# Two pair steps moved ahead of a short convolution, and one operand split per gate tile in place of two, in a two-layer gated-mixer trunk

## The chip, the cores and the metric

The kernel runs on one core of a Trainium2 chip. The metric is the device time of one execution in microseconds (us); three executions of the kernel before gave a median of 1846.69 us.

## What is computed

The state x is 2048 tokens by 1024 features, float32. Layer 0 applies the short-convolution mixer, layer 1 a pooling mixer; after each mixer comes a gated embedding, and a last RMSNorm ends the trunk.

```
h  = rmsnorm(x, g)
b, c, v, z = split(h @ w_in, 4)                    # w_in 1024 x 4096
y  = b * causal_conv3(c * v, w_conv)               # three taps over the tokens, per feature
x  = x + (silu(z) * y) @ w_out                     # first mixer
gate = sigmoid(rmsnorm(x, g2) @ w_gate)
x  = x + gate * (p[0] @ w_proj)                    # gated embedding
...                                                # second mixer and its gate, then the last norm
```

## The kernel before

Features lie on the 128 partitions, tokens along the free dimension. There are four chunks of 512 tokens; `sc` = 0 and 1 handle two chunks each, through all of both layers (line 945 on). So the order of stages is: first mixer (`mixer_a`), its output product, two gates, second mixer (`mixer_b`), its output product, two gates, and all of that once more for `sc` = 1. What stands between the last gates of `sc` = 0 and the first mixer of `sc` = 1 is called the turn.

Every float32 product is made of three matmuls (`mm`, lines 273 to 275): high part of the weight by high part of the operand, high by low, low by high. High and low parts are made in advance: ACT casts a tile to its high part, DVE subtracts it from the tile. For a weight granule of 128x1024 that is lines 116 and 117 (`split_raw`), for an operand lines 301 and 302 (`split_act`) or 307 and 308 (`split_scaled`).

The first mixer's input product is done in the Strassen-Winograd manner over 2x2 blocks (two chunks of tokens, two halves of the features): seven products of sums in place of eight. The seven operand sums are x11, x21, t2, t1, t3, x22 and t4, each in four tiles. `X(name)` (class `Operands`, line 526) returns the four tiles of one and makes those that are still missing; `X.ahead(n)` makes the next n tiles in the order x11, x21, t2, t1, t3, x22, t4. For `sc` = 1 a tile is made by `second_operand` (line 604): `fetch` (lines 599 to 601) loads it from DRAM (`ndr`) into one of the four `n` buffers, and `split_act` splits it into one of the 31 `act` buffers. The `n` buffers also take the embedding tiles of the gates (`pdr`, line 748).

`pair_steps` (line 436) makes two output tiles of the product in three steps, with products of 12 matmuls each:
- step 1: x11 into PSUM tile pa, x21 into pb; ACT copies pa (c1, line 428), DVE adds pb and c1 (m1, line 433)
- step 2: t2 on top of pa, ACT copies pa again (c2); t1 into pc, ACT copies pc (c5)
- step 3: t3 on top of pa, DVE adds pa and c5 (n2); x22 on top of pc, DVE adds pc and c2 (m2); t4 on top of pa

In `mixer_a` (line 467) a loop runs over eight tiles j of 128 features. Each has a c-v pair and a z-b pair. In the program's order, tile j does: steps 2 and 3 of its c-v pair (line 479; step 1 was issued by the tile before, line 505); the products u1 and u2 of c and v (lines 483 and 484, on POOL and DVE); the convolution cv1 and cv2 (line 491 on ACT, then two taps each at line 493 on DVE); every other tile, the sums over the outputs of the two tiles before (`Y.add`, line 498, `combine`); all three steps of its z-b pair (line 502); step 1 of the next c-v pair (line 505); in `sc` = 0 some preparation of sums of the output weights (line 507); the gating (lines 511 to 516). u, cv, c1, m1, c2, c5, n2 and m2 all lie in the ten `wk` buffers.

What sets the order: nothing is ordered by hand but the program itself. The framework hands out the buffers of a pool strictly in the program's order (the first writers of the 784 `wk` tiles stand in that order in the compiled kernel before, without an exception), and within this and the data's own dependences its scheduler puts each engine's instructions in the order in which they become ready by its own reckoning, the earlier in the program first where several are ready. So c1 of the z-b pair, whose buffer comes after those of u2, cv1 and cv2, stands behind the first instruction of cv1 and cv2 in ACT's order, though the product that it copies is done long before. Each engine then runs its list in order. There are seven PSUM banks for products, and four weight granules in the ring `w` (loaded three ahead, `next_granule`, line 262).

In a gate (`gate`, line 770) each of eight tiles k has a product of 24 matmuls, an embedding tile from DRAM, `gate_out` (lines 752 to 755: DVE, ACT, DVE, DVE) and the squares for the next norm (line 328 on ACT, 331 on POOL), and then calls `extra(k)`; for the second layer's gates of `sc` = 0 that is `ahead` (line 970). Behind the second of these gates comes `filler` (line 984), embedding products of chunk 2, whose PSUM tiles are copied on ACT at line 735.

Of the kernel before, what the change touches and what calls it, by code (L numbers as in the profile page):

```python
# [48 lines left out]
def trunk_kernel(ctx: ExitStack, tc: tile.TileContext, xT, xN, pT, wts, par, out):  # L49
# [15 lines left out]
    def wtile():  # L65
        return wk.tile([P, 528], F32, tag="wk", name="wk")
# [5 lines left out]
    def pcol(c):  # L72
        return par_sb[:, c:c + 1]
# [69 lines left out]
    def prepare_sums(layer, i):  # L143

        base = (W_AOUT, W_BOUT)[layer] + 2 * i
        with tc.issue_after(newest[0].ins):
            w11, w12, w21, w22 = (fetch(wts[base + r][:, c * HK:(c + 1) * HK]) for r in range(2) for c in range(2))
        vec(w22, w21, w22, ALU.add)
        vec(w21, w11, w21, ALU.subtract)
        vec(w11, w22, w11, ALU.subtract)  # L150
        vec(w12, w12, w11, ALU.subtract)
        for n, sm in enumerate((w22, w11, w21, w12)):
            nc.sync.dma_start(out=so_dram[layer][:, n, i, :], in_=sm)
# [151 lines left out]
    def split_scaled(h, gcol):  # L305
        a = new_act()
        nc.scalar.activation(out=a[:, 0, :], in_=h, func=AF.Copy, scale=pcol(gcol))  # L307
        nc.vector.scalar_tensor_tensor(out=a[:, 1, :], in0=h, scalar=pcol(gcol), in1=a[:, 0, :].bitcast(F32),  # L308
                                       op0=ALU.mult, op1=ALU.subtract)
        return a  # L310
# [125 lines left out]
    def pair_steps(sc, i, X):  # L436

        pa, pb = psum(), psum()
        w = next_granule(("sum", (sc, i, 0)))
        product(pa, w, 0, X("x11"), True)  # L440
        product(pb, w, HK, X("x21"), True)
        c1 = copied(pa)
        m1 = added(pb, c1)
        yield
        w = next_granule(("sum", (sc, i, 1)))
        product(pa, w, HK, X("t2"), False)
        c2 = copied(pa)
        pc = psum()
        product(pc, w, 0, X("t1"), True)
        c5 = copied(pc)  # L450
        yield
        w = next_granule(("sum", (sc, i, 2)))
        product(pa, w, 0, X("t3"), False)
        n2 = added(pa, c5)
        product(pc, w, HK, X("x22"), False)
        m2 = added(pc, c2)
        w = next_granule(("sum", (sc, i, 3)))
        product(pa, w, 0, X("t4"), False)
        yield m1, m2, pa, n2

    def pair_of(steps):

        for r in steps:
            if r:
                return r

    def mixer_a(sc, X, Y, later):
        def steps(j, i):
            return pair_steps(sc, 2 * j + i, X)

        cv_steps = steps(0, 0)
        due = []
        for j in range(KT):
            zb_steps = steps(j, 1)
            if j == 0:
                next(cv_steps)
                next(zb_steps)
                look[0] = LOOK
            cs1, cs2, v1, v2 = pair_of(cv_steps)
            us = []  # L480
            for t, (c, v) in enumerate(((cs1, v1), (cs2, v2))):
                u = wtile()
                nc.gpsimd.tensor_copy(out=u[:, 0:2], in_=uh[:, j, :] if t == 0 else us[0][:, T:T + 2])
                nc.vector.tensor_tensor(out=u[:, 2:2 + T], in0=v, in1=c, op=ALU.mult)
                us.append(u)
            if sc == 0:
                nc.gpsimd.tensor_copy(out=uh[:, j, :], in_=us[1][:, T:T + 2])
            cvs = []
            for u in us:
                cv = wtile()  # L490
                nc.scalar.activation(out=cv[:, :T], in_=u[:, 0:T], func=AF.Copy, scale=pcol(C_CONV + j))
                for t in (1, 2):
                    nc.vector.scalar_tensor_tensor(out=cv[:, :T], in0=u[:, t:t + T],
                                                   scalar=pcol(C_CONV + 8 * t + j),
                                                   in1=cv[:, :T], op0=ALU.mult, op1=ALU.add)
                cvs.append(cv)
            for args in due:
                Y.add(*args)
            due = []
            if j == KT - 1:  # L500
                Y.begin(later)
            z1, z2, b1, b2 = pair_of(zb_steps)
            if j + 1 < KT:
                cv_steps = steps(j + 1, 0)
                next(cv_steps)
            for i in () if sc else ((), (0,), (1,), (2,), (3,), (4, 5), (6, 7), ())[j]:
                prepare_sums(*divmod(i, KT // 2))
            for t, (z, b) in enumerate(((z1, b1), (z2, b2))):
                cv = cvs[t][:, :T]
                zs = wtile()[:, :T]  # L510
                nc.scalar.activation(out=zs, in_=z, func=AF.Sigmoid)
                nc.vector.tensor_tensor(out=zs, in0=z, in1=zs, op=ALU.mult)
                nc.vector.tensor_tensor(out=cv, in0=cv, in1=zs, op=ALU.mult)
                if j % 2 == t == 0:
                    yt = [acts.tile([P, 2, T], F32, tag="act", name="y") for _ in range(2)]
                nc.vector.tensor_tensor(out=yt[t][:, j % 2, :], in0=b, in1=cv, op=ALU.mult)
            if j % 2:
                due.append((j // 2, yt))
        for args in due:
            Y.add(*args)  # L520
# [29 lines left out]
    def first_operand(x, stats):  # L550

        def make(name, kk):
            n11, n12, n21, n22 = (x[t][2 * kk + r] for r in range(2) for t in range(2))
            if name == "x11":
                normed(n11, n11, 2 * kk, stats[0].rb)
                return split_act(n11)
            if name == "x21":
                normed(n21, n21, 2 * kk + 1, stats[0].rb)
                return split_act(n21)
            if name == "t2":  # L560
                normed(n12, n12, 2 * kk, stats[1].rb)
                normed(n22, n22, 2 * kk + 1, stats[1].rb)
                vec(n12, n22, n12, ALU.subtract)
                vec(n11, n12, n11, ALU.add)
                return split_act(n11)
            if name == "t1":
                vec(n21, n21, n11, ALU.subtract)
                vec(n11, n22, n11, ALU.subtract)
                return split_act(n11)
            return split_act({"t3": n12, "x22": n22, "t4": n21}[name])  # L570
        return make
# [166 lines left out]
    def filler(layer, ch, *between):  # L738

        keys = filler_order(layer, ch)  # L740
        pt = next_granule(keys[0])
        for h in range(2):
            ple_half(layer, ch, pt, next_granule(keys[1 + h]), h)
            for f in between[h:h + 1]:
                f()
# [167 lines left out]
    X = Operands(first_operand(x, stats))  # L913
# [31 lines left out]
    for sc in range(2):  # L945
        chs = (2 * sc, 2 * sc + 1)
        Y = Outputs(2 * sc, (0, 1, 2, 3))
        mixer_a(sc, X, Y, xT[chs[1]])
        filler(*((0, 3) if sc else (1, 0)))
        a, hs, s = mixer_out(0, Y, xT[chs[0]])  # L950
        hooks.extend([s[1].fin1, nop, s[1].fin2])
        ab, ss = ([], []), []
        for t, ch in enumerate(chs):
            def after_gate(k):
                ab[t].append(split_scaled(hs[t][k], G_MIX + 8 + k))
                keep(ch, hs[t], k)

            ss.append(gate(0, ch, a[t], hs[t], s[t], after_gate))
            if t == 0:
                hooks.extend([ss[0].fin1, nop, ss[0].fin2])  # L960
        filler(1, 1 + sc, ss[1].fin1, ss[1].fin2)

        Y = Outputs(2 * sc + 1, (3, 2, 1, 0))
        mixer_b(ab, ss, Y, sc, nop if sc else between_b, h_dram[chs[1]])
        a, hs, s = mixer_out(1, Y, h_dram[chs[0]])
        hooks.extend([s[1].fin1, nop, s[1].fin2])
        if sc == 0:
            X = Operands(second_operand)

        def ahead(k):  # L970
            if sc == 0:
                X.ahead(1 + t)

        for t, ch in enumerate(chs):
            if ch == NCH - 1:
                look[0] = 1
                gate_last(1, ch, a[t], hs[t], s[t])
                break
            g = gate(1, ch, a[t], hs[t], s[t], ahead)
            if t == 0:  # L980
                hooks.extend(finals(ch, hs[t], g))
                continue
            fin1, _, fin2 = finals(ch, hs[t], g)
            filler(0, 2, fin1, fin2)
# [55 lines left out]
```

## Time and profile before

| | us |
|---|---|
| median of three runs | 1846.69 (1844.87 to 1856.14) |
| the profiled execution | 1848.54 |
| its span, first to last instruction | 1846.8 |
| PE busy in the span | 1776.5 |
| DVE busy in the span | 1350.7 |

PE does the matmuls, PEld loads their weights, DVE is the vector engine, ACT the scalar engine, POOL the third elementwise engine, SP only issues DMAs. An L with a number is a line of the kernel. Matmuls overlap: one of 512 columns is shown with 0.39 us, while the next starts 0.23 us after it; so what PE loses at a wait is read from the idle time that the profile gives for it and from the distance of the starts. A name behind an arrow (<-) in square brackets or at the end of a line is what ended the wait.

### The profile page before, as it was taken

Reading aid. Unit: us, or ns where it says so; the run is one execution under the profiler, and the core shown is the slowest. Engines: PE = TensorE matmul, PEld = TensorE weight load, DVE = VectorE, ACT = ScalarE, POOL = GpSimd, SP = SyncE. Lnnn points to the kernel's source line nnn. Section 1 sums busy time; section 2 is a strip of 40 time slices with the busy share of each in tenths; the row PEclk is TensorE's granted clock in tenths of the full one; section 3 lists DMA queues with packets and bytes.
Section 4 is the critical chain, followed back from the end, with each engine's and each line's share of the span. In section 5 each row is a group of like instructions: output and inputs, shape, how many; then the busy total and the mean of one; then the engine's idle time right before and its main releaser. Section 6 shows DMA issues by size and latency. Waiting matters only on the chain.

```text
span 1846.8 us, 22147 instructions
## 1 busy us (share of the span) xinstructions
PE 1776.5 (96%) x8014; PEld 1459.0 (79%) x8014; DVE 1350.7 (73%) x1878; ACT 754.6 (41%) x1141; POOL 233.3 (13%) x218
## 2 busy tenths in 40 slices
PE   8799999989999999999979999999999999999996
PEld 6587777878788888887868877877878888888796
DVE  4886776776988778879786555466698876578975
ACT  6642333344656221345553233234465511135542
POOL 1000000000322010013210000000032300001320
PEclk9999999999999999999999999999999999999998
DMA  9545455667355456853674434246635522265431
GB/s 322 191 146 195 168 205 186 243 232 272 114 194 187 146 198 221 281 198 127 209 239 155 137 103 137 94 146 221 246 126 194 192 109 99 97 224 170 142 114 47
DMA packets 122495, 324.49 MB, mean 176 GB/s; under 512 B 13584, under 2 KB 15632, under 8 KB 122384
## 3 DMA queue, kind: packets, MB, share of 16 engines
q1 hardware_dynamic: 122384, 323.06, 50.8%
q8 instruction: 63, 1.03, 0.2%
q14 instruction: 48, 0.39, 0.1%
HBM read 225.49 MB, written 97.52 MB: 175 GB/s over the span
## 4 chain that ended last, share of the span: by engine, by line
PE 65%; DVE 17%; issue 5%; DMA 5%; ACT 3%; POOL 1%; SPq 1%; DVEq 0%; ACTq 0%; POOLq 0%
PE mm L275 22%; PE mm L273 21%; PE mm L274 21%; DVE w L117 5%; DVE act L302 2%; DMA n<-ndr 2%; DMA n<-in_wts_dram 2%; DVE act L308 2%; ACT w L116 1%; DVE h L699 1%; DMA raw<-in_wts_dram 1%; DVE wk L754 1%; DVE n L548 1%; SPq L601 1%; ACT wk L428 1%
## 5 line engine op out<-in xcount | busy, mean ns | idle before, releaser
L273 PE MATMUL mm<-act,w 128*128 128x512 f32 (+1 forms) x2464 | 942.2, 385 | 19.5 <-ACT wk L428 10.8
L275 PE MATMUL mm<-act,w 128*128 128x512 f32 (+1 forms) x2464 | 935.0, 384 | 12.2 <-DVE w L117 12.0
L274 PE MATMUL mm<-act,w 128*128 128x512 f32 (+1 forms) x2464 | 943.7, 383 | 0.0
L273 PEld LDWEIGHTS mm<-act,w 128*128 128x128 f32 x2464 | 464.2, 188 | 121.3 <-ACT wk L428 16.6
L275 PEld LDWEIGHTS mm<-act,w 128*128 128x128 f32 x2464 | 463.2, 188 | 108.4 <-DVE w L117 17.7
L274 PEld LDWEIGHTS mm<-act,w 128*128 128x128 f32 x2464 | 464.4, 188 | 90.5 <-issue 0.5
L116 ACT CAST w<-raw 128x1024 fp32r<-128x1024 f32 (+1 forms) x283 | 281.6, 1002 | 563.2 <-PE mm L275 474.7
L117 DVE TENSOR_TENSOR w<-raw,w 128x1024 fp32r<-128x1024 f32 (+1 forms) x283 | 336.6, 1194 | 130.8 <-ACT w L116 127.2
L331 POOL TENSOR_TENSOR acc<-acc,wk 128x512 f32<-128x512 f32 x97 | 142.9, 1474 | 490.4 <-ACT wk L328 490.4
L433 DVE TENSOR_TENSOR wk<-mm,wk 128x512 f32<-128x512 f32 x96 | 65.8, 686 | 100.5 <-PE mm L275 100.5
L308 DVE SCALAR_TENSOR_TENSOR act<-h,par_sb,act 128x512 fp32r<-128x512 f32 x96 | 103.8, 1084 | 19.9 <-ACT act L307 17.9
L328 ACT ACTIVATE wk<-h 128x512 f32<-128x512 f32 (+1 forms) x126 | 75.3, 600 | 93.6 <-DVE h L755 93.2
L307 ACT ACTIVATE act<-h,par_sb 128x512 fp32r<-128x512 f32 x96 | 68.9, 718 | 72.7 <-DVE h L699 72.7
L699 DVE TENSOR_TENSOR h<-mm,h 128x512 f32<-128x512 f32 x112 | 75.9, 682 | 26.7 <-PE mm L275 20.7
L302 DVE TENSOR_TENSOR act<-n,act 128x512 fp32r<-128x512 f32 x112 | 76.3, 710 | 22.8 <-ACT act L301 22.7
L428 ACT COPY wk<-mm 128x512 f32<-128x512 f32 x96 | 53.0, 585 | 94.9 <-PE mm L275 94.9
L301 ACT CAST act<-n 128x512 fp32r<-128x512 f32 x112 | 65.7, 619 | 57.3 <-DMA n<-ydr 27.6
L669 DVE TENSOR_TENSOR wk<-wk 128x526 f32<-128x526 f32 (+5 forms) x80 | 55.5, 693 | 2.4
L352 POOL TENSOR_TENSOR r<-ms,nhalf 128x8 f32<-128x8 f32 x18 | 33.1, 1837 | 186.5 <-DVE ms L350 186.5
L684 ACT ACTIVATE wk<-wk 128x512 f32<-128x512 f32 x32 | 20.2, 630 | 78.0 <-DVE wk L682 77.9
L753 ACT ACTIVATE wk<-wk 128x512 f32<-128x512 f32 (+1 forms) x72 | 41.3, 579 | 21.6 <-DVE wk L752 21.4
L682 DVE TENSOR_TENSOR wk<-mm,rb 128x512 f32<-128x512 f32 x32 | 22.0, 688 | 37.6 <-PE mm L275 37.6
(124 smaller groups left out, 1296.1 us busy)
## 6 DMA issues: line engine op xcount, KB each, us to landing
raw<-in_wts_dram SPq DMA_DIRECT2D x154, 512.0 KB, 3.4
n<-ydr SPq DMA_DIRECT2D x84, 256.0 KB, 4.5
ydr<-y SPq DMA_DIRECT2D x32, 512.0 KB, 3.3
raw<-in_wts_dram SPq DMA_DIRECT2D x64, 256.0 KB, 3.3
raw<-sdo SPq DMA_DIRECT2D x32, 512.0 KB, 6.3
raw<-sda SPq DMA_DIRECT2D x32, 512.0 KB, 3.7
pdr<-wk SPq DMA_DIRECT2D x56, 256.0 KB, 4.0
n<-pdr SPq DMA_DIRECT2D x56, 256.0 KB, 3.5
```

The costliest lines, as they stand in the source:

```text
L116: nc.scalar.copy(out=hi[:, c], in_=raw[:, c])
L117: eng.tensor_tensor(out=lo[:, c], in0=raw[:, c], in1=hi[:, c].bitcast(F32), op=ALU.subtract)
L273: nc.tensor.matmul(out=ps, lhsT=wh, rhs=ah, start=first, stop=False, skip_group_check=skip)
L274: nc.tensor.matmul(out=ps, lhsT=wh, rhs=al, start=False, stop=False, skip_group_check=skip)
L275: nc.tensor.matmul(out=ps, lhsT=wl, rhs=ah, start=False, stop=last, skip_group_check=skip)
L302: nc.vector.tensor_tensor(out=a[:, 1, :], in0=y, in1=a[:, 0, :].bitcast(F32), op=ALU.subtract)
L307: nc.scalar.activation(out=a[:, 0, :], in_=h, func=AF.Copy, scale=pcol(gcol))
L308: nc.vector.scalar_tensor_tensor(out=a[:, 1, :], in0=h, scalar=pcol(gcol), in1=a[:, 0, :].bitcast(F32), op0=ALU.mult, op1=ALU.subtract)
L328: nc.scalar.activation(out=sq, in_=h, func=AF.Square)
L331: (eng or nc.gpsimd).tensor_tensor(out=acc, in0=acc, in1=sq, op=ALU.add)
L428: nc.scalar.copy(out=c, in_=ps)
L699: nc.vector.tensor_tensor(out=hs[t][k], in0=ps, in1=hs[t][k], op=ALU.add)
```

## The change

In `mixer_a`, behind the products u1 and u2 and ahead of the convolution, step 1 and step 2 of the z-b pair are issued (for the first tile step 2 alone, since its step 1 was issued before the loop's body); line 502 then runs what is left, step 3. In the second layer's gates of `sc` = 0, `ahead` makes one operand tile for each gate tile in both gates; before, it made one in the first gate and two in the second. So 16 of the 28 tiles are made there in place of 24; the four of t3 and the four of x22 are made when step 3 of the first c-v pair of `sc` = 1 asks for them, as the four of t4 were before.

```diff
@@ mixer_a @@
             if sc == 0:
                 nc.gpsimd.tensor_copy(out=uh[:, j, :], in_=us[1][:, T:T + 2])
+            if j:
+                next(zb_steps)
+            next(zb_steps)
             cvs = []
             for u in us:
                 cv = wtile()
@@ trunk_kernel @@
         def ahead(k):
             if sc == 0:
-                X.ahead(1 + t)
+                X.ahead(1)
```

## Rows read from the trace of the kernel before

**Rows 1.** The page, part 1: busy time, share of the span, instructions

```profile
PE 1776.5 (96%) x8014; PEld 1459.0 (79%) x8014; DVE 1350.7 (73%) x1878; ACT 754.6 (41%) x1141; POOL 233.3 (13%) x218
```

**Rows 2.** Busy time by stretch: PE, PEld, DVE, ACT, POOL (instructions), clock, DMA

```profile
105.00:400.00 295.00, 282.11 (x1217) 226.47 (x1217) 212.16 (x302) 99.98 (x141) 20.26 (x23) 1.00 0.57 201
...
850.00:965.00 115.00, 104.08 (x445) 83.68 (x444) 94.31 (x127) 61.27 (x95) 27.59 (x19) 0.99 0.62 204
965.00:1280.00 315.00, 307.52 (x1336) 250.48 (x1335) 175.89 (x236) 106.05 (x155) 8.30 (x17) 0.99 0.41 137
...
600.00:700.00 100.00, 100.00 (x439) 82.05 (x438) 71.55 (x114) 24.98 (x36) 8.49 (x14) 1.00 0.51 180
```

**Rows 3.** Waits of PE, 105 to 405 us: us, times, longest us

```profile
PE mm L273 <- ACT wk L428: 5.8, 8, 2.2
PE mm L275 <- DVE w L117: 5.7, 7, 2.1
PE mm L273 <- ACT w L116: 1.4, 3, 0.5
```

**Rows 4.** Waits of PE, 965 to 1280 us

```profile
PE mm L273 <- ACT wk L428: 5.1, 5, 2.8
PE mm L273 <- ACT w L116: 2.3, 5, 0.5
```

**Rows 5.** Timeline of ACT, 148 to 160 us: start, us, instruction, idle before

```profile
148.46 1.05 ACT L116 CAST w<-raw 128x1024 fp32r<-128x1024 f32 x1 [3.64 <-PE mm L275]
149.91 1.34 ACT L491 ACTIVATE wk<-wk,par_sb 128x512 f32<-128x512 f32 x2 [0.41 <-DVE wk L484]
151.15 0.56 ACT L428 COPY wk<-mm 128x512 f32<-128x512 f32 x1
159.06 1.07 ACT L428 COPY wk<-mm 128x512 f32<-128x512 f32 x2 [7.35 <-PE mm L275]
```

**Rows 6.** Timeline of PE, the same stretch

```profile
149.56 0.50 PE L273 MATMUL mm<-act,w 128*128 128x512 f32 x1 [0.46 <-ACT w L116]
...
150.36 0.39 PE L274 MATMUL mm<-act,w 128*128 128x512 f32 x1
151.60 0.50 PE L275 MATMUL mm<-act,w 128*128 128x512 f32 x1 [0.85 <-DVE w L117]
...
159.70 0.50 PE L273 MATMUL mm<-act,w 128*128 128x512 f32 x1 [0.50 <-ACT wk L428]
```

**Rows 7.** Timeline of PE, last tile of the first mixer, second time

```profile
1267.87 0.79 PE L273 MATMUL mm<-act,w 128*128 128x512 f32 x1 [2.84 <-ACT wk L428]
1268.46 0.63 PE L274 MATMUL mm<-act,w 128*128 128x512 f32 x1
1268.88 0.63 PE L275 MATMUL mm<-act,w 128*128 128x512 f32 x1
```

**Rows 8.** Waits of PE at the turn, 905 to 965 us

```profile
PE mm L273 <- ACT wk L735: 5.1, 1, 5.1
PE mm L273 <- DVE wk L752: 3.8, 2, 2.0
```

**Rows 9.** Timeline of ACT at the turn

```profile
936.18 0.62 ACT L301 CAST act<-n 128x512 fp32r<-128x512 f32 x1 [2.71 <-DMA out_dram<-h]
...
945.02 0.62 ACT L301 CAST act<-n 128x512 fp32r<-128x512 f32 x1 [3.11 <-DMA n<-ndr]
...
959.70 2.03 ACT L735 COPY wk<-mm 128x512 f32<-128x512 f32 x4
```

**Rows 10.** Durations ns (min/median/max) by line: the second half of an operand's split; a tap of the convolution

```profile
L302 DVE TENSOR_TENSOR act<-n,act x27: 676/683/1414, 859.8 to 962.9; 128x512 fp32r<-128x512 f32 x27
...
L493 DVE SCALAR_TENSOR_TENSOR wk<-wk,par_sb x32: 734/742/753, 115.8 to 396.9; 128x512 f32<-128x512 f32 x32
```

**Rows 11.** Timeline of DVE, behind the first boundary of rows 5

```profile
161.11 1.22 DVE L117 TENSOR_TENSOR w<-s,w 128x1024 fp32r<-128x1024 f32 x1 [5.11 <-ACT w L116]
```

## The prediction, made before the changed kernel was run

> **What bounds the kernel now.** I read the page first: PE is busy for 1776.5 of 1846.8 us, 96%, so nothing but PE's lost time can be won [rows 1]. Busy time hides part of the loss, so I next read the kernel by stretches and counted matmuls. In 600 to 700 us PE never waits and starts 439 matmuls, one in 0.228 us. At that rate 105 to 400 us (first mixer, first time) would hold 1294; it holds 1217, so some 77, or 17.6 us, are missing. The turn (850 to 965) misses 59, 13.5 us; the first mixer's second time (965 to 1280) misses 46, 10.5 us [rows 2]. A few records may be lacking, so these are upper bounds: some 41 us lie in the stretches that the change touches, and the other stages matter little.
>
> The waits of PE say what ends these stops. In the first mixer it waits for three things: an ACT copy of PSUM (line 428), the low part of a weight granule (DVE, line 117), and its high part (ACT, line 116): 5.8, 5.7 and 1.4 us in the first time [rows 3], 5.1, none and 2.3 us in the second [rows 4]. The timeline of one tile's boundary shows how they hang together. At 148.46 the t4 product of the c-v pair is done. ACT casts the next pair's granule, waits for u1, starts cv1 and cv2, and only then copies c1 of the z-b pair (151.15) [rows 5]. PE, whose next product t2 waits for c1, turns to the next c-v pair, whose granule is just being split: it stops at 149.56 for the high part and at 151.60 for the low part, does all it can of that pair, then t2, and at 159.70 stops again, since t3 waits for the copy c2 of the PSUM tile that t2 has just left, with nothing to put between [rows 6]. Buffers go out in the program's order, so c1 cannot stand ahead of cv1 and cv2.
>
> **The change part by part.** A wait costs PE more than its idle time: at 151.60 it idled 0.85 us, but start follows start by 1.24 us in place of 0.228, a loss of 1.01; I add 0.16 us to every wait [rows 2, 6].
>
> *Steps 1 and 2 ahead of the convolution.* No instruction is added or removed, and PE's own list need not change. c1 now needs only u2's buffer before it, so it comes off ACT straight behind the granule's cast, two activations earlier: 151.15 - 149.91 = 1.24 us [rows 5]. Then t2 is ready before the low part of the new granule is, goes first, and hides the DVE's split under 2.7 us of its own (12 x 0.228); the 20 matmuls left of the next pair's step 1 (4.6 us) then lie between t2 and t3 and hide c2 (0.6 us, half of the pair at 159.06).
> - First time, tiles 1 to 6: of the seven waits for line 117 six lie at boundaries, 5.7 less the 2.1 of the longest, which is elsewhere: 3.6 + 6 x 0.16 = 4.6 us. Of the eight waits for line 428, six: 5.8 less the last tile's 2.2 and 0.7, that is 2.9 + 6 x 0.16 = 3.9 us [rows 3]. Together 8.5 us. The high-part waits stay.
> - Second time: of five waits for line 428 three lie at boundaries, 5.1 less the last tile's 2.8 and 0.7: 1.6 + 3 x 0.16 = 2.1 us [rows 4]. The five high-part waits stay.
> - Last tile, both times: there is no next pair to turn to, so PE waits for c1 in any case, but 1.24 us less, 2.5 us in all. After the longest wait (2.84 us) the starts stand 0.42 us apart in place of 0.228 [rows 7], the lower of the engine's two clock levels, 1.2 of 2.4 GHz; over some eight starts that cost 1.5 us, and after the 2.2 us wait of the first time the trace shows none of it. With the wait cut to 1.6 us I count half of it back: 0.8 us. Sum 3.3 us.
>
> What it moves: cv1 and cv2 now stand behind c5, some 5 us later, and their four taps (4 x 0.742 = 3.0 us [rows 10]) with them; n2, m2 and the splits of the z-b pair's step 3 queue behind them on DVE, and t4 waits for n2. The loads on SP's list keep their program order. What hides it: behind the boundary shown DVE idles for 5.11 us, up to 161.11 [rows 11], more than the taps take. So the cost lies between nothing (taps in that idle time; no gain, since gating waits for PE's t4 anyway) and 3.0 us for each of 16 tiles, 48 us (none of it hidden). The idle row is the nearest; I take 0.1 us a tile, 1.6 us.
>
> Sum for this part: 8.5 + 2.1 + 3.3 - 1.6 = 12.3 us.
>
> *One operand tile in place of two.* PE loses at the turn 3.8 us waiting for line 752 and 5.1 us for line 735, three waits [rows 8], with 0.16 each 9.4 us, and about 1.5 us more at the low clock behind the longest, as in [rows 7]: 10.9 us. Both are PSUM tiles that nobody empties: gate_out runs late on DVE and ACT, and the filler's copies stand behind it on ACT. The timeline says why: ACT stands still 2.71 us at a cast of an operand tile whose `act` buffer an output transfer still reads, and 3.11 us at another whose load has not landed, with gate_out's sigmoids queued behind [rows 9]. Both kinds come from making two tiles per gate tile: by my count of the 31 `act` buffers only the eighth and later tiles of the second gate need a buffer that waits for the output; after the change there are eight. Eight casts (0.62 us, [rows 9]) and eight subtractions (0.68 us, [rows 10]) leave the stretch, 5.0 us on ACT and 5.4 us on DVE, and the 3.11 us wait. If gate_out ends 8 us sooner, the first copy of line 735 comes at 951.7 and not at 959.70; PE, were it not held up, would need that bank near 950.7, so a wait of about 1.6 us stays: 9.3 us won at most, nothing at least (if the queue is late for another reason).
>
> The eight tiles of t3 and x22 are now made later, between the gates' end and step 3 of the first c-v pair (20 us on). Casts and subtractions amount to 5.0 and 5.4 us; in 965 to 1280 us ACT is idle two thirds of the time and DVE 44% [rows 2]. They also bring eight DMAs on SP's list behind the granules', and ACT can again stand still at a load. Cost: nothing to 10.4 us (both sums, nothing hidden). I take 3.8, nearer to nothing because there is idle time on both engines. Net 5.5 us.
>
> The Trainium skill speaks against this part: "DMA: Bandwidth & Descriptors", section "Rules for kernel authors", says to overlap a transfer with compute by issuing it early and waiting for it late. The trace shows loads issued early whose tiles then block ACT's list [rows 9], so here I side with the trace; by the rule the second part would win nothing, the first rival below.
>
> Together 17.8 us. The profiled execution took 1848.54 us, 1.7 us more than its span, and would come to 1830.7. It stands 1.85 us above the median of 1846.69, so I forecast 1829 us as the median.
>
> **The rivals.**
> - *The turn gives nothing back*: the eight tiles come too late and PE waits for t3 what it no longer waits for PSUM. For it: in [rows 9] a load's landing, too, stops ACT. Against it: 20 us of room. Only the first part is left: 1846.7 - 12.3 = 1834, or a little more.
> - *The boundaries stay as they are*: the scheduler, with another reckoning of the copies, still puts the next pair's 20 matmuls ahead of t2. For it: at the boundary of [rows 6] it put them first though c1 was ready soon after. Against it: c1 now leads by 1.24 us. Then only the turn counts: 1841.
> - *Slower: the convolution is late.* If t2 still comes after the 20 matmuls, c5, cv1 and cv2 come 5 us later still, the taps fall together with the splits (1.22 us each) and n2 misses t4. The point from which it decides: taps and one split, 3.0 + 1.2, exceed the x22 product that covers them, 2.7 us; beyond that PE stands for 1.5 us in each of 14 tiles, 21 us. With the boundaries' gain gone and the turn's 5.5 us kept: 1846.7 + 21 - 5.5 = 1862. Against it: the 5.11 us of [rows 11].
> - *All of it and more*: no price for the convolution (+1.6), the turn's full 9.3 (+3.8), and the eight high-part waits hidden as well (3.7 + 8 x 0.16 = 5.0): 28 us, 1818.
>
> **How the numbers follow.** Forecast 0.56, own range 1822 to 1836; turn gives nothing 0.13; boundaries stay 0.12; slower 0.07; more 0.12. For the range I go from 1818 to 1845, which holds all but the slower rival and the ends. A measurement of this kernel tells about 1% from no change, here below 1828.2 or above 1865.2. Faster: all of the last rival and nearly half of the forecast's own range, 0.38. Slower by over 1%: half of the slower rival, 0.04. Within 1%: 0.58.
>
> **What would show it.** Right: at the tile boundaries ACT's line 428 ahead of line 491, PE's waits for line 428 in the first mixer down from 10.9 us to about 4 (the last tiles alone), those for line 117 in 105 to 405 us down to about 2, those for line 116 unchanged; at the turn no wait for line 752 and under 2 us for line 735. Wrong: waits of PE for line 433 or 117 new in step 3 (the late convolution), waits for line 301 or 302 near the first t3 (late operands), or line 428 earlier with PE's waits unchanged.

## The result: 16.9 us less, where 17.7 were forecast

| | before | after |
|---|---|---|
| median of five runs each, us | 1848.82 | 1831.90 |
| the profiled execution, us | 1848.54 | 1832.44 |
| its span, us | 1846.8 | 1830.4 |

The ratio is 0.9898, with a 95% interval of 0.988 to 0.9916, that is 15.5 to 22.2 us; it is not the quotient of the two medians, which is 0.9908. The forecast was 1829.0 us, against a median of before that then stood at 1846.69. The change adds three lines to `mixer_a`: what was line 491, 493, 735 or 752 is 494, 496, 738 or 755 in the profile after.

PE's busy time is nearly the same and its share is higher, beside [rows 1]:

```profile
PE 1774.8 (97%) x8014; PEld 1461.9 (80%) x8014; DVE 1355.1 (74%) x1878; ACT 754.1 (41%) x1141; POOL 233.5 (13%) x218
```

The stretches of [rows 2], in the changed kernel (columns as there):

```profile
105.00:400.00 295.00, 287.27 (x1252) 233.51 (x1251) 218.46 (x309) 102.20 (x146) 21.30 (x23) 1.00 0.57 203
850.00:965.00 115.00, 109.30 (x465) 88.82 (x465) 95.27 (x129) 62.13 (x96) 25.65 (x18) 0.96 0.66 218
965.00:1280.00 315.00, 309.96 (x1357) 253.98 (x1357) 185.33 (x246) 113.67 (x166) 5.09 (x15) 1.00 0.43 145
```

The first stretch holds 35 matmuls more (1252 against 1217), at 0.228 us each 8.0 us. The clock of the second stretch has fallen from 0.99 to 0.96; more on that at the end. The later windows are shifted against the kernel before, so the gain is better read between like instructions. For that I took from DVE's timeline the start of the product u1 of tiles 0 and 7 in each pass, and from PE's the matmul of line 362 with which the norm ahead of each layer's two gates ends (499.16 us in the kernel before, 491.07 after). So the turn in this table and in the experiments runs from the norm ahead of the second layer's gates to u1 of tile 0 and contains these gates:

| us | before | after | change | forecast |
|---|---|---|---|---|
| start to u1 of tile 0 | 112.9 | 112.7 | -0.2 | 0 |
| first pass, tile 0 to tile 7 | 279.1 | 272.6 | -6.5 | with the next: |
| its last tile and the output product, to the norm | 107.1 | 105.8 | -1.3 | -8.9 |
| from there to the norm ahead of the second layer's gates | 354.8 | 354.8 | 0 | 0 |
| from there to u1 of tile 0: the turn | 140.3 | 136.9 | -3.4 | -5.5 |
| second pass, tile 0 to tile 7 | 270.8 | 268.5 | -2.3 | with the next: |
| its last tile and the output product, to the norm | 108.5 | 105.8 | -2.7 | -3.3 |
| the rest | 473.2 | 473.4 | +0.2 | 0 |

(The price of 1.6 us put on the late convolution is spread evenly over both passes in the last column.) All of the gain lies where it was looked for; its shares differ.

PE's waits in the first pass, 105 to 405 us, beside [rows 3]: us, times, longest us.

```profile
PE mm L275 <- DVE w L117: 3.8, 2, 2.4
PE mm L273 <- ACT w L116: 2.3, 5, 0.5
PE mm L273 <- ACT wk L428: 1.6, 2, 0.9
```

At the turn, 905 to 965 us, beside [rows 8]:

```profile
PE mm L273 <- ACT wk L738: 3.6, 1, 3.6
PE mm L273 <- DVE wk L755: 2.1, 1, 2.1
```

In the second pass, 965 to 1280 us, beside [rows 4]:

```profile
PE mm L273 <- ACT w L116: 2.7, 6, 0.5
PE mm L273 <- ACT wk L428: 2.3, 2, 1.6
```

The waits for line 428 have fallen from thirteen (10.9 us) to four (3.9 us), all in the two last tiles; at a boundary there is none left. The seven waits for the low part of a granule have become two. The waits for its high part have grown from eight to eleven.

The same boundary as in [rows 5], on ACT:

```profile
146.35 1.06 ACT L116 CAST w<-raw 128x1024 fp32r<-128x1024 f32 x1 [2.50 <-PE mm L275]
147.31 0.57 ACT L428 COPY wk<-mm 128x512 f32<-128x512 f32 x1
152.24 1.07 ACT L428 COPY wk<-mm 128x512 f32<-128x512 f32 x2 [4.36 <-PE mm L275]
153.20 1.35 ACT L494 ACTIVATE wk<-wk,par_sb 128x512 f32<-128x512 f32 x2
```

c1 now comes straight behind the cast, and the convolution behind c2 and c5. On PE, four matmuls with the high part of the next pair's granule run from 148.42; then t2 starts at 149.32 and hides the low part's split; the 20 matmuls that are left of that pair's step 1 start from 152.04 on, t3 at 156.58. There is no idle time in the stretch. (At most of the other boundaries PE stops for 0.46 us for the cast.) The taps (line 496, at 153.97 on DVE) stand where DVE had nothing else to do.

### The profile page after: what moved, and what is told of

The parts are those of the page before. It is cut to its first block, busy times and chain, and to the rows that moved or that the text cites. A ratio compares the mean times of both kernels' runs of the same rounds, so it can differ in the third digit from the quotient of the medians.

```text
span 1830.4 us, 22127 instructions
## 1 busy us (share of the span) xinstructions
PE 1774.8 (97%) x8014; PEld 1461.9 (80%) x8014; DVE 1355.1 (74%) x1878; ACT 754.1 (41%) x1141; POOL 233.5 (13%) x218
## 4 chain that ended last, share of the span: by engine, by line
PE 70%; DVE 14%; issue 5%; DMA 3%; ACT 3%; POOL 1%; SPq 0%; DVEq 0%; ACTq 0%; POOLq 0%
PE mm L273 23%; PE mm L275 23%; PE mm L274 23%; DVE w L117 3%; DVE act L302 2%; DVE act L308 2%; ACT w L116 2%; DVE h L702 1%; DMA n<-in_wts_dram 1%; DMA n<-ndr 1%; DVE wk L757 1%; POOL r L352 1%; DMA sdo<-n 1%; DVE h L788 1%; DVE h L551 0%
## 5 line engine op out<-in xcount | busy, mean ns | idle before, releaser
L273 PE MATMUL mm<-act,w 128*128 128x512 f32 (+1 forms) x2464 | 941.7, 385 | 12.3 <-ACT w L116 8.4
L496 DVE SCALAR_TENSOR_TENSOR wk<-wk,par_sb 128x512 f32<-128x512 f32 x64 | 44.1, 748 | 34.8 <-ACT wk L494 34.8
```

Of the source, the lines that this page charges most:

```text
L273: nc.tensor.matmul(out=ps, lhsT=wh, rhs=ah, start=first, stop=False, skip_group_check=skip)
```

## The experiments

Each ratio is against the kernel before on the same chip: its median was 1853.89 us for x1 to x4 and 1849.39 for the others. Gains in us are (1 - ratio) times that. Stage times come from one trace each, and the trace of the kernel before was taken in an execution of 1848.54 us; so for x1 to x4 the spans of the traces differ from it by 3 to 6 us less than the ratios say (x1: 8.8 us against 15.2).

### x1_steps_only: the pair steps without the operand change

```diff
         def ahead(k):
             if sc == 0:
-                X.ahead(1)
+                X.ahead(1 + t)
```

(against the changed kernel)

> The two steps ahead of the convolution, with two operand tiles per gate tile as before the change. My theory (the gain is c1's place in the order of the wk buffers, most of it in the first mixer): some 13.5 us faster than before, ratio 0.9925 to 0.993, PE's waits for line 428 in both passes of the first mixer about 4 us in place of 10.9, the turn's three waits (line 752 and 735 of the kernel before, 3.8 and 5.1 us) as before. Rival A (the turn carries half or more of the 17 us): ratio 0.9955 or above.

Measured: 1838.19 us, ratio 0.9918 (0.9905 to 0.9931), that is 15.2 us, somewhat over the 12.3 of the forecast; in the traces the two passes with their last tiles give 12.4. Rival A, by which the turn carries half, falls. The first mixer's waits are those of the changed kernel but for one more for line 117 (three, 4.2 us), and its passes take 272.9 and 268.6 us, as after the change. The turn became 2.8 us longer (143.1 us); why was not followed further.

### x2_ahead_only: the operand change without the pair steps

```diff
         def ahead(k):
             if sc == 0:
-                X.ahead(1 + t)
+                X.ahead(1)
```

(against the kernel before)

> One operand tile per gate tile, the steps where they were. My theory by the two traces (the turn gave back 2.7 us, since the scheduler brings the splits of t3 and x22 forward into the same stretch): 2 to 4 us faster, ratio 0.998 to 0.999, PE's waits at the turn some 5.7 in place of 8.9 us, line 428 in the first mixer unchanged at 10.9 us. Rival A (the turn carries half or more): 8 us or more faster, ratio below 0.9957. Rival B (the second edit only pays with the first): no faster than before, 0.9995 to 1.003.

Measured: 1846.02 us, ratio 0.9963 (0.9951 to 0.9975), 6.9 us. The turn took 136.2 us in place of 140.3. Beside [rows 8], one of PE's two waits for line 752 is gone and the other is 1.3 us; the longest, for line 735, stayed at 5.0 us. The waits of the second pass stayed as in [rows 4]. So the two parts don't need each other, and the rival by which the turn gives nothing falls; the gain is more than the 2 to 4 us expected and less than rival A's 8. In the traces x1's passes (12.4 us) and x2's turn (4.1 us) add up to the 16.4 us between the spans of before and after. The two gains add up to 22 us; the whole change's interval is 15.5 to 22.2 us, so they agree with it no better than that. One caution for stage times: x2 leaves the first mixer as it was, yet its tile 0 came 3.0 us earlier and the pass behind it took 2.8 us longer (281.9 us), so a single start can shift by that much.

### x3_step1_only: only step 1 goes ahead of the convolution

```diff
             if j:
                 next(zb_steps)
-            next(zb_steps)
             cvs = []
```

(against the changed kernel)

> The changed kernel, but only step 1 of the z-b pair stands ahead of the convolution (for the first tile nothing, since its step 1 was issued already); step 2 is behind it again. My theory (what counts is that c1 no longer needs the buffers of cv1 and cv2): as fast as the changed kernel within 2 us, ratio to before 0.989 to 0.991, since c1 comes as early. Rival C (moving step 2 matters: its granule loads and splits, its copies c2 and c5, stand earlier than the taps): the gain in the first mixer falls by half or more, ratio 0.993 or above.

Measured: 1830.11 us, ratio 0.9875 (0.9862 to 0.9887). The whole gain is there with step 1 alone. PE's waits in the first pass:

```profile
PE mm L273 <- ACT w L116: 2.7, 6, 0.5
PE mm L273 <- ACT wk L428: 2.3, 2, 1.6
PE mm L275 <- DVE w L117: 0.7, 1, 0.7
```

c1 is in step 1, and its place is what counts; moving c2 and c5 past the convolution as well adds nothing. The two long waits for line 117 went down to 0.7 us.

### x4_own_cv_buffers: the program's order of before, other buffers

```diff
-    wk = ctx.enter_context(tc.tile_pool(name="wk", bufs=10))
+    wk = ctx.enter_context(tc.tile_pool(name="wk", bufs=8))
+    cvp = ctx.enter_context(tc.tile_pool(name="cvp", bufs=2))
...
-                cv = wtile()
+                cv = cvp.tile([P, 528], F32, tag="cv", name="cv")
```

(against the kernel before; its lines are one higher)

> The kernel before, in its own program order and with two operand tiles per gate tile; only the two convolution tiles come from two buffers of their own, and wk has eight in place of ten. If the order of the buffers is the cause, c1 needs only u2's buffer here too, though it stands behind the convolution in the program: PE's waits for line 428 in the first mixer fall from 10.9 to 4 to 7 us, and the time to 0.993 to 0.998 of before, unless eight wk buffers cost time in the second mixer, which the stretches would show. Rival D (the program's order itself, that is the priority of c1 over line 491, is the cause): waits for line 428 stay at 10 to 11 us.

Measured: 1843.31 us, ratio 0.9949 (0.9935 to 0.9963), 9.5 us from the buffers alone. The boundary of [rows 5] on ACT:

```profile
145.05 1.06 ACT L117 CAST w<-raw 128x1024 fp32r<-128x1024 f32 x1 [0.74 <-PE mm L276]
146.01 0.72 ACT L492 ACTIVATE cv<-wk,par_sb 128x512 f32<-128x512 f32 x1
146.63 0.57 ACT L429 COPY wk<-mm 128x512 f32<-128x512 f32 x1
147.09 0.72 ACT L492 ACTIVATE cv<-wk,par_sb 128x512 f32<-128x512 f32 x1
```

With cv out of the pool, c1 passes cv2, though the program still asks for it later. That is the mechanism of the forecast shown by itself: the order in which one pool's buffers are handed out put c1 behind the convolution. The eight `wk` buffers cost nothing in the second mixer (354.7 us from norm to norm, as against 354.8). It is only a part, as the waits of the first pass show:

```profile
PE mm L274 <- ACT wk L429: 5.7, 7, 2.2
PE mm L274 <- ACT w L117: 2.3, 5, 0.5
PE mm L276 <- DVE w L118: 1.2, 1, 1.2
```

The seven waits for a low part (5.7 us) became one of 1.2, but those for c1 and c2 stayed at 5.7 us. In the second pass they went from five (5.1 us) to two (3.0 us). Together that is 8.7 us, between the 4 to 7 expected and rival D's 10 to 11. With c1 still behind cv1, not every boundary turns; whether the rest is the program's own order or other buffers, x4 does not tell.

### x8_all_steps: all three steps ahead of the convolution

```diff
-            if j:
-                next(zb_steps)
-            next(zb_steps)
+            z1, z2, b1, b2 = pair_of(zb_steps)
             cvs = []
...
-            z1, z2, b1, b2 = pair_of(zb_steps)
             if j + 1 < KT:
```

(against the changed kernel)

> The changed kernel with step 3 ahead of the convolution as well, so that cv1 and cv2 need the buffers of n2 and m2 before them and start some 10 us later still. It sizes the slack behind the late convolution. My theory (the taps have room, 3 us of work in tiles of 39 us, as long as they end before the gating needs them): the taps now meet the end of t4, so 0.5 to 2 us a tile are lost, 8 to 30 us slower than the changed kernel, ratio 0.994 to 1.006. Rival H (slack is plenty): as fast as the changed kernel, within 3 us.

Measured: 1827.40 us, ratio 0.9886 (0.9867 to 0.9905). At the boundary shown the first taps now come at 163.04, 9 us later than in the changed kernel and behind both sums of the z-b pair's step 3 (the second at 161.76); still PE's waits of the first pass hold nothing new:

```profile
PE mm L273 <- ACT w L116: 2.3, 5, 0.5
PE mm L273 <- ACT wk L428: 1.6, 2, 0.9
PE mm L275 <- DVE w L117: 0.6, 1, 0.6
```

A convolution that is later still costs nothing. The 1.6 us put down for it were not there, and the slower rival has no ground here: rival H holds, and the expectation of 8 to 30 us failed.

### x5_step1_before_u: step 1 ahead of the products u1 and u2 too

```diff
             cs1, cs2, v1, v2 = pair_of(cv_steps)
+            if j:
+                next(zb_steps)
             us = []
...
-            if j:
-                next(zb_steps)
             next(zb_steps)
             cvs = []
```

(against the changed kernel)

> The changed kernel with step 1 of the z-b pair one place further ahead: in front of u1 and u2 (step 2 stays behind them). My theory: c1 needs no buffer of u2 now and is copied before the c-v pair's t4 ends, so t2 runs across the boundary and hides the granule's cast. PE's waits for line 116 in the first mixer (11 of 0.46 us in the changed kernel) and for c1 in the two last tiles (0.94 and 1.62 us) vanish: 5.0 + 1.8 us plus the low clock's share behind the last one, 7 to 9 us faster than the changed kernel, ratio to before 0.985 to 0.9865. Rival E (u1 and u2, now behind c1 and m1 on DVE, come late and with them cv and the gating): no faster than the changed kernel, 0.989 to 0.992, with waits elsewhere.

Measured: 1814.90 us, ratio 0.9817 (0.9801 to 0.9832): 33.8 us less than before, twice the gain of the change. In 105 to 405 us PE waits for nothing; in 965 to 1280 us one wait is left:

```profile
PE mm L273 <- ACT wk L428: 0.7, 1, 0.7
```

Busy time of the two passes' stretches (columns as in [rows 2]):

```profile
105.00:400.00 295.00, 294.99 (x1299) 243.12 (x1299) 227.54 (x324) 109.06 (x158) 28.20 (x23) 1.00 0.61 211
965.00:1280.00 315.00, 314.32 (x1387) 259.96 (x1386) 191.82 (x256) 116.61 (x170) 14.26 (x15) 1.00 0.48 162
```

The first now holds 1299 matmuls, as many as 295 us can hold at 0.228 us (1294). The boundary on ACT shows why:

```profile
142.52 1.05 ACT L116 CAST w<-raw 128x1024 fp32r<-128x1024 f32 x1 [7.26 <-PE mm L275]
143.47 0.58 ACT L428 COPY wk<-mm 128x512 f32<-128x512 f32 x1
...
147.73 1.06 ACT L116 CAST w<-raw 128x1024 fp32r<-128x1024 f32 x1 [2.51 <-PE mm L275]
```

In the changed kernel c1's buffer still came after u1's and u2's, which are filled only when the c-v pair's step 3 is nearly through: c1 came at 147.31, when t4 (from 143.43 on) was done. Now it comes at 143.47, before t4 starts (144.81). t2 starts at 148.44 without a gap on PE, which reaches the next pair's granule only at 152.52, and by then its high part, cast at 147.73, and its low part, split from 151.07, are there. So the waits for line 116, taken as fixed in the forecast, go with the others, and the gain is about twice the 7 to 9 us expected. The last tiles gain too, 4.2 us in the first pass and 1.9 in the second over the changed kernel.

### x6_hold_operands: the moved operand tiles held back

```diff
+    hold = [None]
+
     def second_operand(name, kk):
-        return split_act(fetch(n_dram[kk][:, SLOT[name], :]))
+        n = fetch(n_dram[kk][:, SLOT[name], :])
+        if name in ("t3", "x22", "t4"):
+            with tc.issue_after(hold[0].ins):
+                return split_act(n)
+        return split_act(n)
...
-            nc.scalar.copy(out=e, in_=ps)
+            c = nc.scalar.copy(out=e, in_=ps)
...
+            if k == 3:
+                hold[0] = c
```

(against the changed kernel; the splits of t3, x22 and t4 are put behind the filler's fourth copy, line 744 here)

> The changed kernel, with the casts of the t3, x22 and t4 tiles of the second pass held on ACT behind the fourth PSUM copy of the filler. My theory (at the turn the splits that were moved came back into the same stretch and stand in front of the filler's copies): PE's waits at the turn fall from 5.7 to 1 to 3 us, 3 to 5 us faster than the changed kernel with the slow clock behind the longest wait gone, ratio 0.987 to 0.9885. Rival F (the queue at the turn is gate_out's own chain and the output's arithmetic on DVE): waits stay at 5 us or more, ratio as the changed kernel. Rival G (held splits come too late for t3): a wait for line 301 or 302 in front of the first t3, no faster or slower.

First, what it is about. ACT and then DVE at the turn of the changed kernel:

```profile
940.60 0.62 ACT L301 CAST act<-n 128x512 fp32r<-128x512 f32 x1 [1.29 <-DMA n<-ndr]
942.03 0.63 ACT L756 ACTIVATE wk<-wk 128x512 f32<-128x512 f32 x1 [0.81 <-DVE wk L755]
...
945.85 1.23 ACT L301 CAST act<-n 128x512 fp32r<-128x512 f32 x2 [1.11 <-DMA n<-ndr]
...
947.51 2.03 ACT L738 COPY wk<-mm 128x512 f32<-128x512 f32 x4
```

```profile
939.64 1.76 DVE L302 TENSOR_TENSOR act<-n,act 128x512 fp32r<-128x512 f32 x1
941.32 0.68 DVE L755 TENSOR_TENSOR wk<-mm,rb 128x512 f32<-128x512 f32 x1
```

Counted in order, the casts of line 301 from 940.60 on are the 18th and later of the 28, and only 16 tiles are made ahead (with the hold, exactly 16 casts stand ahead of the filler's copies, without it 21): they are tiles of t3 and x22, which the program now asks for only in step 3 of the first c-v pair, after the filler. Nothing that the program says holds them there; the scheduler put them ahead of the last gate tile's `gate_out` and the filler's copies, and ACT again stands still at their loads.

Measured: 1830.57 us, ratio 0.9897 (0.988 to 0.9915). The waits of PE at the turn with the splits held back:

```profile
PE mm L273 <- DVE wk L763: 2.3, 1, 2.3
PE mm L273 <- ACT wk L744: 1.5, 2, 0.8
```

5.7 us of waits became 3.8, and the turn 135.0 us in place of 136.9; the time of the kernel can't be told from that of the change. So the splits explain much of the wait for the filler's copies, but the 3 to 5 us expected did not come, and rival F (5 us of waits or more) does not hold either. The turn's length does not decide it: x3 and x8, with nothing held back, took 136.4 and 135.3 us.

The wait for `gate_out` itself is 2.1 us without the hold and 2.3 with it. It goes with one split on DVE ahead of `gate_out`'s first operation: 1.76 us at 939.64 above, 1.75 us in x6 (at 941.39, a tile that is not held). In x3 the split at this place is as short as others, and PE waits 0.4 us:

```profile
938.59 0.69 DVE L302 TENSOR_TENSOR act<-n,act 128x512 fp32r<-128x512 f32 x1
```

Why it is long in the one kernel and short in the other stays open.

### x7_both: x5 and x6 together

The two diffs above in one kernel.

> Both of the last two edits. If they are independent: the sum of their gains, 10 to 14 us faster than the changed kernel, ratio 0.982 to 0.985. If one takes the other's cover: less than the larger of the two plus 2 us.

Measured: 1813.99 us, ratio 0.9809 (0.9794 to 0.9824). The turn is 1.9 us shorter than in x5 (135.8 against 137.7 us); the two kernels' intervals overlap almost wholly, so between them nothing is decided. The two gains cannot be seen to add up, since x6 alone shows none in time. Both beat the kernel before and the change.

## Why the prediction was right, and where it was off

**The boundaries: right in mechanism.** c1 led the convolution, t2 went before the 20 matmuls, c2 was hidden, and no boundary wait for line 428 was left: exactly four remain, 3.9 us against "about 4". x3 and x4 show that it was c1's place, and x4 that the buffers had set a good part of it. "The boundaries stay as they are" falls.

**The low parts: nearly.** "Down to about 2" measured 3.8 us in two waits. They are not at the boundary treated in the forecast, but in two late tiles where a granule's split stands on DVE behind the gating. One of these waits was there before (2.1 us at 376.96, now 1.4 at 370.19); the other is new, and close to the sign that the forecast named for a late convolution. DVE and then PE there:

```profile
325.73 1.29 DVE L516 TENSOR_TENSOR wk<-wk 128x512 f32<-128x512 f32 x2
...
327.66 0.68 DVE L519 TENSOR_TENSOR y<-mm,wk 128x512 f32<-128x512 f32 x1
328.26 1.22 DVE L117 TENSOR_TENSOR w<-raw,w 128x1024 fp32r<-128x1024 f32 x1
```

```profile
329.53 0.50 PE L275 MATMUL mm<-act,w 128*128 128x512 f32 x1 [2.36 <-DVE w L117]
```

x3 and x8, one with the convolution earlier and one with it later, have only 0.7 and 0.6 us of such waits. So the late convolution is not their cause; why DVE's order falls out this way in the one program and not in the others stays open.

**The high parts: the step that called them unchanged failed.** There are eleven, not eight: 5.0 us against 3.7, with 0.16 for each of the three more a loss of 1.8 us. The step took the boundaries that had no such wait to stay without one. At tile 2, before and then after:

```profile
188.42 1.05 ACT L116 CAST w<-raw 128x1024 fp32r<-128x1024 f32 x1 [3.19 <-PE mm L275]
```

```profile
186.01 1.05 ACT L116 CAST w<-raw 128x1024 fp32r<-128x1024 f32 x1 [3.64 <-PE mm L275]
187.11 0.50 PE L273 MATMUL mm<-act,w 128*128 128x512 f32 x1 [0.46 <-ACT w L116]
```

Before, the cast started 1.4 us ahead of PE's first matmul with this granule (189.81); now it starts 0.5 us ahead of the time at which PE is free for it (its last matmul before starts at 186.27), and the cast takes 1.05 us. In the first pass these waits cost 1.2 us and the low parts 1.8 us against the forecast, while 0.8 us for the convolution were not paid. That makes 6.7 of the 8.9 us forecast; 7.8 came, so about 1 us is not accounted for.

**The last tiles: under-sized.** The second pass's last tile was given 1.24 us and half of the clock's 1.5. Its segment gave 2.7. The wait of [rows 7] is now 1.62 us, and the starts behind it stand at full pace:

```profile
1252.84 0.50 PE L273 MATMUL mm<-act,w 128*128 128x512 f32 x1 [1.62 <-ACT wk L428]
1253.17 0.39 PE L274 MATMUL mm<-act,w 128*128 128x512 f32 x1
```

1.24 and the whole 1.5 make 2.7: by this one trace the term that was halved should have been counted in full.

**The late convolution:** 1.6 us forecast, none found (x8). The idle row of [rows 11] was the right one to go by, and nothing should have been added to it.

**The turn: the term that was mis-sized.** "If gate_out ends 8 us sooner ... a wait of about 1.6 us stays" measured 5.7 us in two waits, and the turn gave 3.4 us of 5.5. The step that failed is the one that moved the eight tiles to "between the gates' end and step 3": what comes later in the program need not come later on the engines. Of the 4.1 us of waits above the forecast, x6 takes back 1.9. The rest is open: the wait for `gate_out` goes with the long split, but in x3, where the split is short, PE waits 4.5 us for the copies instead. The 3.8 us put down for those tiles in the second pass did not appear there (PE has no wait for line 301 or 302): they were made at the turn, and that is one reason why 3.4 us came there of the 9.3 counted.

The rule of the Trainium skill that was weighed against this part ("DMA: Bandwidth & Descriptors", section "Rules for kernel authors": issue a transfer early, wait for it late) would have had this part win nothing. By x2 it won 6.9 us. The forecast's reason, loads whose tiles block ACT's list, is not shown by that: from 860 to 985 us ACT stood 18.0 us at casts waiting for such loads in the kernel before and 20.3 us in x2, while the 5.8 us at casts waiting for output transfers vanished. What the fewer casts and subtractions in the gates are worth by themselves was not tried, and the moved loads were still issued early.

So a sum of 17.8 came out at 16.4 us between the spans, because misses of both signs nearly cancelled: 1.1 us too little in the first pass, 2.1 at the turn, 1.7 too much in the second pass. The mechanism of the boundaries was right; that the sum came so close was in part luck.

## What to carry to other kernels

Where buffers of a pool are handed out in program order, an operation that frees a PSUM tile belongs in the program ahead of every tile whose data come later than its own; ask of each buffer what the ones before it wait for (the products u waited for the last sums of their pair, which mattered as much as the convolution, and the change stopped one step short of them). Putting work later in the program moves it later only if a dependence or a buffer holds it there: look in the trace for where the scheduler put it. When several kinds of wait stand at one boundary, count what PE can do between two of them rather than price each alone, since one reordering can hide them all.

## What was not expected

**One more place up was worth as much again as the whole change**: 1814.9 us. The waits for casts, splits and PSUM copies, 20.3 us in both passes of the kernel before [rows 3, 4], hung together, and all but 0.7 us of them went with c1's place.

**The length of a wait alone does not say whether PE's clock falls.** Four stretches of the changed kernel (granted clock in the third column from the right), around the waits that began there:

```profile
942.00:945.00 3.00, 2.49 (x6) 1.49 (x6) 3.00 (x6) 2.18 (x3) 0.00 (x0) 0.60 0.72 180
948.00:952.00 4.00, 3.87 (x9) 3.13 (x10) 1.90 (x3) 4.00 (x8) 1.03 (x1) 0.50 0.94 314
329.00:333.00 4.00, 3.47 (x15) 2.90 (x16) 4.00 (x7) 0.00 (x0) 0.00 (x0) 1.00 0.74 296
...
1252.00:1256.00 4.00, 3.02 (x12) 2.17 (x12) 1.83 (x2) 0.89 (x3) 0.18 (x1) 1.00 0.87 313
```

After 2.12 us (942.06) and 3.58 us (948.13) at the turn the clock fell to or stood at its half, 1.2 of 2.4 GHz; after 2.36 us (329.53) and 1.62 us (1252.84) in the first mixer it was full. In the starts at the turn this is plain:

```profile
942.06 0.50 PE L273 MATMUL mm<-w 128*128 128x512 f32 x1 [2.12 <-DVE wk L755]
942.39 0.45 PE L274 MATMUL mm<-w 128*128 128x512 f32 x1
942.63 0.63 PE L275 MATMUL mm<-w 128*128 128x512 f32 x1
```

The starts go from 0.24 us apart to 0.43, the next standing at 943.06, some 0.6 us after the wait has ended. In the kernel before, two waits of 1.80 and 1.96 us at the same place left the clock full. From these rows the shorter waits are the safer ones, but 2.12 and 2.36 us stand the wrong way round, and what else decides was not tried. In x6, too, 2.33 us at this place are followed by starts 0.43 apart. It cost some of the turn's gain: twelve starts there stand about 0.43 apart, against six before; at 0.2 us each that is 1.2 us.
